# Second mixer of a hybrid decoder: the in-projection of seven heads in pairs of units, by seven half-size block products a pair

## Chip, cores and metric

The kernel runs on one core of one Trainium2 chip. The metric is device time in microseconds (us): the median of 3 runs before the change is 1518.07 us (1518.05 to 1518.93). A second number is the span of the profiled execution, from the first to the last instruction of the core.

## The reference, cut to what matters

Four sub-layers on 544 tokens (512 of a prompt, 32 of eight samples) with a model width of 1024: a Mamba-2 mixer, an MLP, an HGRN2 mixer and a second MLP, each with an RMS norm ahead and a residual add behind. The change touches the HGRN2 mixer:

```python
def hgrn_mixer(u, state, lb, w_in, norm_w, w_out):
    proj = (u @ w_in).astype(jnp.float32)
    q = jax.nn.silu(proj[..., :HGRN_F])
    fz = proj[..., HGRN_F:2 * HGRN_F]
    v = proj[..., 2 * HGRN_F:2 * HGRN_F + D_MODEL]
    g = proj[..., 2 * HGRN_F + D_MODEL:]
    logf = jnp.logaddexp(jax.nn.log_sigmoid(fz), jnp.log(jnp.maximum(lb, LB_FLOOR)) + jax.nn.log_sigmoid(-fz))
    k = (1.0 - lb) * jax.nn.sigmoid(-fz)
    ...
    o, s = hgrn_chunk_scan(q..., k..., v..., logf..., state)
    o = group_rmsnorm(o.reshape(bt, L, D_MODEL), norm_w, HGRN_N_HEADS) * jax.nn.silu(g)
    return o.astype(u.dtype) @ w_out, s
```

`u` is the normed residual, (tokens, 1024); `w_in` is (1024, 4096): q, f, v and g of 8 heads with 128 columns each. The scan runs per head.

## The kernel before

**Units and products.** The residual lies transposed in eight tiles `x[k]` of 128 x 544 (features by tokens). Weights come in units `W[u]` of 128 x 1024 f32 (512 KB): the 128 output columns of one block for all eight k-blocks. For precision a unit is split into a high part `whi` (rounded to fp32r by ScalarE, L199) and a low part `wlo` (raw minus high, VectorE, L200), in halves of 512 columns; the operand is split the same way into `uh`/`ul`. A unit takes, per k-block and half of the tokens (272), three matmuls: high by high, high by low, low by high: 8 x 3 x 2 = 48. The accumulators `ps` (pool `acc`) are two; smaller PSUM tiles come from `mx`, four. Raw units have three buffers, split halves four.

**Loads and splits.** Lists `loads` and `jobs` hold the order of all units. `load_next` (L173) issues the next load; `conv_unit` splits the next unit, a few ahead of its use. For some units ("by load") the low part is made otherwise: ScalarE writes the negative of the raw unit, rounded to the type of the tile, and GpSimd issues DMAs that add the raw weights from memory to it (`accum_op=ADD`).

**The MLPs** (`_mlp`, `seventh`) already work on pairs of units: the 2 x 2 blocks (two units by two halves of k, against two halves of k by two halves of the tokens) are multiplied by seven products of half size, named p1, p2, n6, q7, n5, p3 and q4, at slots 0, 1, 3, 4, 6, 9 and 12 of a pair, the next pair seven slots later (`SLOTS`). Their weight operands are sums of blocks (`v`, `s2`, `a22`), made by accumulating loads and by VectorE; their token operands are sums as well.

**The HGRN2 mixer** (`hgrn`) before the change: 32 units, four a head (q, f, v, g), each by `product` (48 matmuls) and `project`, which multiplies the accumulator by the row scale `hn_rb` of the RMS norm on VectorE. The operands `uh`/`ul` hold x times the norm's weight, unscaled, so they are ready before the row scale is. `head` then makes sigmoids, K and the gate. Two background queues run work beside the products: `levels` (a scan over chunk sizes 1 to 64 by doubling) and `states` (chunk states, sample states, output, group norm by `newton`, transposes, gate, split into `oh`/`ol`). `tick` counts six product steps and lets a queue step when its pace (`PACE_LEVELS`, `PACE_STATES`) is used up. At the end the out-projection takes 8 units, first with heads 0 to 3, then with heads 4 to 7. Each engine runs its instructions in the order that the program fixes; GpSimd (POOL) issues all rounding and accumulating DMAs from one in-order stream, SyncE (SP) the plain ones.

Of the kernel before, what the change touches and what calls it, by code (L numbers as in the profile page):

```python
# [16 lines left out]
P = 128  # L17
# [27 lines left out]
PACE_LEVELS, PACE_STATES = 1.8, 1.6  # L45
# [42 lines left out]


# [12 lines left out]
def trunk(ctx: ExitStack, tc: tile.TileContext, io):  # L102
# [60 lines left out]
    by_load = {ub + i for ub in (U_MLP, U_MLP2) for i in (1, 2, 3, 4, 5, 6, 8, 9)}  # L163
    plans = [plan_mlp(U_MLP, False)]
    for u in range(U_HGRN_IN, U_MLP2):
        loads.append(("u", u))
        jobs.append((("u", u), len(loads) - 1))
# [5 lines left out]
    def load_next():  # L173
        kind, u = loads[state["load"]]
        state["load"] += 1
        if kind == "u":
            raw = wraw.tile([P, 1024], F32, tag="raw", name=f"raw{u}")
            nc.sync.dma_start(raw, io["W"][u])
        elif kind == "a22":
            raw = mp["w"].tile([P, 512], F32, tag="a22", bufs=1, name=f"a22_{u}")  # L180
            nc.sync.dma_start(raw, io["W"][u + 1][:, 512:])
        else:
# [4 lines left out]
            for c in (0, 512):  # L187
                nc.gpsimd.dma_start(raw[:, c : c + 512], io["W"][u + 1][:, :512], accum_op=ADD)  # L188
# [13 lines left out]
    def conv_unit():  # L202
# [4 lines left out]
        with tc.high_priority() if u > 2 else ExitStack():  # L207
            while state["load"] <= min(at + (3 if mp else 2 if "w" in sp else 1), len(loads) - 1):
                if loads[state["load"]][0] != "u" and not mp:
                    break  # L210
                load_next()
        with tc.high_priority() if u > 2 and not mp else ExitStack():
            if kind == "u":
# [12 lines left out]
                if added(u + 1):  # L226
                    added_low(u + 1)
            else:
# [11 lines left out]
    def added_low(u):  # L240
# [5 lines left out]
        for a in range(2):  # L246
            nc.gpsimd.dma_start(lows[u][a], io["W"][u][:, 512 * a : 512 * a + 512], accum_op=ADD)

# [20 lines left out]
    def halves_of(job):  # L269
        return 2 if job[0][0] == "u" else 1  # L270
# [54 lines left out]
    def products(ps, w, ops, first, last, c0=0, step=P, run=0):  # L325
# [7 lines left out]
        for i, (k, j) in enumerate(order):  # L333
# [7 lines left out]
            if i % 6 == 5:  # L341
# [854 lines left out]
    def hgrn(then):  # L1196
        es = ExitStack()
        cp = es.enter_context(tc.tile_pool(name="h_const", bufs=1, reuse_waits="tile"))
        pool = es.enter_context(tc.tile_pool(name="h_pool", bufs=2, reuse_waits="tile"))
# [5 lines left out]
        idm = cp.tile([P, NS], F32, name="idm")  # L1205
        nc.sync.dma_start(idm, io["sel"])
# [5 lines left out]
        nc.sync.dma_start(seqrow, io["seqrow"])  # L1212
        sel = cp.tile([P, NS], F32, name="h_sel")
# [20 lines left out]
        background(rstd_steps(1.0 / D, "hn", res, nt, wait=3), "hn", wait=3)  # L1234

        def product(u):
            w = unit(u)
            ps = acc_tile(f"ps{u}")
            products(ps, w, uops, True, True)
            return ps  # L1240

        def project(u, name, ps=None):
            ps = product(u) if ps is None else ps
            t = pool.tile([P, T], F32, tag="ev", bufs=3, name=f"{name}{u}")
            nc.vector.tensor_tensor(v3(t), ps[:, :, :HF], v3(res[0]), MUL)
            return t

        def levels(h, QQ, K, f, d):


            q, Q = QQ[:, 0], QQ[:, 1]
            ac = pool.tile([P, 4, NS], F32, tag="ac", name=f"ac{h}")
# [421 lines left out]
```

## Time and profile before

| what | value |
|---|---|
| median of 3 runs | 1518.07 us |
| profiled execution, time | 1518.08 us |
| profiled execution, span | 1516.2 us |
| mean granted TensorE clock | 0.995 |
| second mixer, in-projection | 814.7 to 1087.4 us |
| second mixer, out-projection | 1087.4 to 1146 us |
| windows of that stage | PE full, DMA share 0.25 to 0.36 |

The page of the profile gives busy time by engine, a chain of waits followed back from the last instruction, groups of instructions by line and tile, and the issues of DMAs with their time to landing. Windows give the busy time of each engine, the granted clock and the DMA share in a chosen stretch. Busy times of matmuls overlap, since they are pipelined.

### The profile page before, as it was taken

Reading aid. Unit: us, or ns where it says so; the run is one execution under the profiler, and the core shown is the slowest. Engines: PE = TensorE matmul, PEld = TensorE weight load, DVE = VectorE, ACT = ScalarE, POOL = GpSimd, SP = SyncE. Lnnn points to the kernel's source line nnn. Section 1 sums busy time; section 2 is a strip of 40 time slices with the busy share of each in tenths; the row PEclk is TensorE's granted clock in tenths of the full one; section 3 lists DMA queues with packets and bytes.
Section 4 is the critical chain, followed back from the end, with each engine's and each line's share of the span. In section 5 each row is a group of like instructions: output and inputs, shape, how many; then the busy total and the mean of one; then the engine's idle time right before and its main releaser. Section 6 shows DMA issues by size and latency. Waiting matters only on the chain. (4 is left out here: it accounts for less than half of the span.)

```text
span 1516.2 us, 33202 instructions
## 1 busy us (share of the span) xinstructions
PE 1489.2 (98%) x13124; PEld 1426.4 (94%) x13124; DVE 1274.6 (84%) x2532; ACT 882.8 (58%) x1740; POOL 200.2 (13%) x289
## 2 busy tenths in 40 slices
PE   8999999999999999999999999999999999999996
PEld 7998889898999999999999999999999999999996
DVE  7989899878777879898898788888877989888895
ACT  5685756757347658575775333333336658576673
POOL 3112111120012111110100000000003111111101
PEclk9999999999999999999999999999999999999998
DMA  6366557483556576665653222233228667575741
GB/s 199 100 198 181 148 131 207 125 227 108 143 157 153 127 181 159 167 173 149 161 152 115 73 87 87 89 111 92 87 90 195 138 166 177 143 190 135 185 113 67
DMA packets 91451, 215.45 MB, mean 142 GB/s; under 512 B 16480, under 2 KB 20480, under 8 KB 91296
## 3 DMA queue, kind: packets, MB, share of 16 engines
q1 hardware_dynamic: 64688, 161.85, 32.9%
q0 software_dynamic: 25344, 50.34, 19.4%
q8 instruction: 103, 1.69, 0.4%
q10 hardware_dynamic: 1264, 1.14, 0.2%
q14 instruction: 52, 0.43, 0.1%
HBM read 196.12 MB, written 17.18 MB: 141 GB/s over the span
## 5 line engine op out<-in xcount | busy, mean ns | idle before, releaser
L199 ACT CAST whi<-raw 128x512 fp32r<-128x512 f32 x194 | 119.4, 617 | 205.9 <-PE ps L337 149.0
L200 DVE TENSOR_TENSOR wlo<-raw,whi 128x512 fp32r<-128x512 f32 x194 | 134.0, 692 | 28.4 <-ACT whi L199 26.0
L188 POOL DMA_DIRECT2D v<-in_W x94 | 82.9, 1020 | 465.2 <-DVE fl_p L200 135.4
L337 PE MATMUL ps<-uh_s,whi 128*128 128x272 f32 x576 | 124.4, 297 | 4.2 <-DVE BC L535 2.4
L337 PE MATMUL ps<-ul_s,whi 128*128 128x272 f32 x576 | 120.1, 289 | 0.0
L337 PE MATMUL ps<-uh,whi 128*128 128x272 f32 x512 | 112.4, 300 | 0.0
L337 PE MATMUL ps<-ul,whi 128*128 128x272 f32 x512 | 106.8, 289 | 0.0
L337 PE MATMUL ps<-uh,wlo 128*128 128x272 f32 x512 | 106.3, 289 | 0.0
L337 PEld LDWEIGHTS ps<-uh_s,whi 128*128 128x128 f32 x576 | 90.2, 188 | 11.9 <-issue 8.5
L337 PEld LDWEIGHTS ps<-ul_s,whi 128*128 128x128 f32 x576 | 90.4, 188 | 0.6 <-issue 0.3
L200 DVE TENSOR_TENSOR fl_p<-raw,fh_p 128x512 fp32r<-128x512 f32 x94 | 64.2, 690 | 29.1 <-ACT fh_p L199 25.6
L337 PE MATMUL ps<-uh_s,wlo 128*128 128x272 f32 x576 | 85.1, 288 | 0.0
L337 PEld LDWEIGHTS ps<-uh,whi 128*128 128x128 f32 x512 | 80.8, 189 | 3.7 <-issue 1.4
L337 PEld LDWEIGHTS ps<-ul,whi 128*128 128x128 f32 x512 | 80.4, 188 | 0.2
L337 PEld LDWEIGHTS ps<-uh,wlo 128*128 128x128 f32 x512 | 80.0, 188 | 0.2 <-issue 0.2
L199 ACT CAST fh_p<-raw 128x512 fp32r<-128x512 f32 x94 | 57.6, 620 | 38.0 <-PE pp L1108 20.2
L337 PEld LDWEIGHTS ps<-uh_s,wlo 128*128 128x128 f32 x576 | 77.2, 188 | 1.0 <-issue 0.8
L223 ACT CAST whi<-raw 128x512 fp32r<-128x512 f32 x66 | 40.6, 618 | 50.3 <-PE ps L337 21.0
L528 DVE SCALAR_TENSOR_TENSOR cacc<-pre,vh,cacc 128x568 f32<-128x568 f32 x72 | 57.9, 804 | 5.8 <-ACT cacc L526 5.3
L337 PE MATMUL po<-yh,whi 128*128 128x272 f32 x256 | 55.7, 298 | 1.2 <-ACT yh L199 1.2
L1108 PE MATMUL pc_q<-m_th,fh_q 128*128 128x272 f32 x192 | 55.3, 288 | 0.0
L1108 PE MATMUL pc_q<-m_th,fl_q 128*128 128x272 f32 x192 | 55.3, 288 | 0.0
(492 smaller groups left out, 5162.7 us busy)
## 6 DMA issues: line engine op xcount, KB each, us to landing
raw<-in_W SPq DMA_DIRECT2D x175, 512.0 KB, 4.0
v<-in_W SPq DMA_DIRECT2D x94, 256.0 KB, 4.1
v<-in_W POOLq DMA_DIRECT2D x94, 256.0 KB, 5.5
wlo<-in_W POOLq DMA_DIRECT2D x66, 256.0 KB, 6.1
a<-in_W SPq DMA_DIRECT2D x47, 256.0 KB, 4.1
w<-cum_d POOLq DMA_DIRECT2D x16, 512.0 KB, 7.5
st<-in_ssm_in SPq DMA_DIRECT2D x16, 512.0 KB, 4.5
out_ssm_s<-st SPq DMA_DIRECT2D x16, 512.0 KB, 6.1
```

The costliest lines, as they stand in the source:

```text
L188: nc.gpsimd.dma_start(raw[:, c : c + 512], io["W"][u + 1][:, :512], accum_op=ADD)
L199: nc.scalar.copy(hi, raw)
L200: (eng or nc.vector).tensor_tensor(lo, raw, hi.bitcast(F32), SUB)
L223: nc.scalar.copy(hi[a], c)
L337: nc.tensor.matmul(ps[:, h, :HF], block(a, c0 + k * step), o[:, h * HF : (h + 1) * HF], start=(first and i == 0), stop=(last and i == len( ...
L528: nc.vector.scalar_tensor_tensor(acc, pre[:, i : i + 568], vh[:, wc + 24 * i : wc + 24 * i + 1], acc, MUL, ADD)
L1108: nc.tensor.matmul(ps, block(w, k * P), o, start=(name_ in ("p1", "p2", "q7") and k == 0 and j == 0), stop=(k == 3 and j == 2), skip_group ...
```

## The change

**What it does.**
- Head 0 keeps its four whole units, with their low parts by load, and with all high products of a unit ahead of its low ones (`run=8`). So do the 8 units of the out-projection, by load.
- Heads 1 to 7 become 14 pairs, (q, f) and (v, g), by the seven products of `SLOTS`: 7 x 12 = 84 matmuls a pair in place of 96.
- The first unit of each pair is loaded by GpSimd straight into an fp32r tile ("c": the load rounds), so that p1 and p2 need no split; their low part `lo` (one buffer) is ScalarE's negative and one accumulating load of 512 KB, started by `low_ahead`, for the next pair along with n5 of the pair before. The sums `v` are made by two accumulating loads a pair, `s2` by a VectorE sum and an accumulating load. Five forms a pair are split as before.
- The row scale goes into the operands: `operands` makes n = x * weight * scale for the eight tiles, splits them (`b1`, `b2`), and makes the sums t1 to t4 in `th` and `tl`; `split_sums` splits these. Results leave PSUM by ScalarE copies (`s`, `sv`, `sw`) and half-width VectorE sums.
- The group norm's sums come from ScalarE (`accum_out`), and its power -1/2 from GpSimd (`pow`), in place of a VectorE reduction and `newton`. K is scaled on ScalarE. Paces are longer, several tiles have one buffer in place of two, and the split gate of heads 4 to 7 waits for the last pair's p1 and p3 (`late`), since it reuses the operands' tiles.

```diff
-PACE_LEVELS, PACE_STATES = 1.8, 1.6
+PACE_LEVELS, PACE_STATES = 2.6, 2.2
...
     by_load = {ub + i for ub in (U_MLP, U_MLP2) for i in (1, 2, 3, 4, 5, 6, 8, 9)}
+    by_load |= set(range(U_HGRN_IN, U_HGRN_IN + 4)) | set(range(U_HGRN_OUT, U_MLP2))
...
+    for i, u in enumerate(hgrn_pairs):
+        loads += [(kind, v) for kind, j in (("v", i), ("c", i + 1), ("va", i), ("a22", i)) for v in hgrn_pairs[j : j + 1]]
...
+        elif kind == "c":
+            raw = wraw.tile([P, 1024], F32, tag="raw", name=f"raw{u}").bitcast(F32R)
+            nc.gpsimd.dma_start(raw, io["W"][u])
...
+        elif kind == "va":
+            raw = None
+            for c in (0, 512):
+                nc.gpsimd.dma_start(loaded["v", u][:, c : c + 512], io["W"][u + 1][:, :512], accum_op=ADD)
...
+    def low_ahead(u):
+        hi = loaded["c", u]
+        lo = mp["w"].tile([P, 1024], F32R, tag="lo12", bufs=1, name=f"lo{u}")
+        nc.scalar.activation(lo, hi.bitcast(F32), AF.Copy, scale=-1.0)
+        nc.gpsimd.dma_start(lo, io["W"][u], accum_op=ADD)
+        lows[u] = lo
+
+    def pair_form(name, u):
+        i = pair_at[u]
+        if name in ("p1", "p2"):
+            c = slice(0, 512) if name == "p1" else slice(512, 1024)
+            return [loaded["c", u][:, c]], [lows[u][:, c]]
+        v = loaded["v", u]
+        if name == "n6":
+            s2 = mp["w"].tile([P, 512], F32, tag="s2", bufs=1, name=f"s2_{u}")
+            nc.vector.tensor_tensor(s2, v[:, 512:], loaded["a22", u], ADD)
+            loaded["s2", u] = s2
+        raw = {"n6": ("s2", 0), "q7": ("v", 512), "n5": ("v", 0), "p3": ("s2", 0), "q4": ("a22", 0)}[name]
...
+        split(raw, hi, lo)
+        if name == "q7":
+            nc.gpsimd.dma_start(loaded["s2", u], io["W"][u][:, 512:], accum_op=ADD)
+        if name == "n5" and i + 1 < len(hgrn_pairs):
+            low_ahead(hgrn_pairs[i + 1])
...
-        pool = es.enter_context(tc.tile_pool(name="h_pool", bufs=2, reuse_waits="tile"))
+        pool = es.enter_context(tc.tile_pool(name="h_pool", bufs=1, reuse_waits="tile"))
...
-        background(rstd_steps(1.0 / D, "hn", res, nt, wait=3), "hn", wait=3)
+        def operands():
+            yield from rstd_steps(1.0 / D, "hn", res, nt, wait=3)
+            yield 3
...
+                nc.vector.scalar_tensor_tensor(n[-1], x[j], vec[:, v0 + j : v0 + j + 1], res[0], MUL, MUL)
...
+                split(b11, *bo)
+                fops["p1", k] = bo
+                yield 1.3
...
+                split(n[1], *bo)
...
+                yield 1
...
+                nc.vector.tensor_tensor(t1, b11, b12, SUB)
+                nc.vector.scalar_tensor_tensor(t2, t1, -1.0, b22, MUL, SUB)
+                nc.vector.tensor_tensor(t3, b12, b22, SUB)
+                nc.vector.tensor_tensor(t4, b21, t2, ADD)
...
+                yield 1.4
+
+        def split_sums():
+            for k, t, (n1, n2) in sorted(sums, key=lambda e: e[0]):
...
+                split(t, *bo)
...
+                yield 0.5
...
+        def seventh(name, u):
+            if name == "p1":
+                t = acc_tile(f"hp{u}")
+                banks[u] = {"a": t[:, 0, :HF], "c": t[:, 1, :HF]}
...
+            hi, lo = take((name, u))
+            n = 0
+            for k in range(4):
+                oh, ol = fops[name, k]
+                for j, (w, o) in enumerate(((hi, oh), (hi, ol), (lo, oh))):
+                    nc.tensor.matmul(
...
+                    n += 1
+                    if n == 6:
+                        tick()
...
-            nc.vector.tensor_reduce(ms, o2, mybir.AxisListType.X, ADD)
+            for c in range(4):
+                nc.scalar.activation(o2[:, c], po[:, c * P : (c + 1) * P], AF.Square, accum_out=ms[:, c : c + 1])
...
-            r = newton(ms, 5)
+            r = pool.tile([P, 5], F32, tag="or", bufs=2, name=f"or{h}")
+            nc.gpsimd.tensor_tensor(r, ms, half, ALU.pow)
...
-        for h in range(8):
-            head(u, h)
-            u += 4
...
+        background(operands(), "hn", wait=3)
+        first = [product(u0 + i) for i in range(2)]
+        while not res:
+            step(queues[0])
+        for i in range(2):
+            project(u0 + i, first[i])
+        for i in range(2, 4):
+            project(u0 + i, product(u0 + i))
+        drain("hn")
+        background(split_sums(), "hs", q=1)
+        for name, u in hgrn_forms:
+            if name == "n6" and u == hgrn_pairs[0]:
+                drain("hs")
+            seventh(name, u)
```

**Where instructions stand.** Three places follow. In all of them, names carry a number behind the tile's own; `hn_` is the mixer's norm.

VectorE at unit 0's projection, before: behind the last step of the row scale come a weight split and the projection of q (`qz` from the accumulator `ps`), then that of f.

```order
L366 SCALAR_TENSOR_TENSOR hn_rb<-hn_rb 128x136
L200 TENSOR_TENSOR wlo_0_10787<-raw_10524,whi_0_10785 128x512
L1245 TENSOR_TENSOR qz_10768<-ps_10636,hn_rb 128x544
L1245 TENSOR_TENSOR fz_10773<-ps_10711,hn_rb 128x544
L1442 TENSOR_TENSOR q_10770<-qz_10768,q_10770 128x544
```

The same place after; the rows begin with the eighth behind the last step of the row scale (`n` are the scaled operands, `b1l`, `b2l` low parts, `th`, `tl` sums).

```order
L1326 SCALAR_TENSOR_TENSOR hn_n_10765<-x,vec,hn_rb 128x544
L1342 TENSOR_TENSOR hn_tl_10754<-hn_n_10727,hn_th_10753 128x272
L1326 SCALAR_TENSOR_TENSOR hn_n_10767<-x,vec,hn_rb 128x544
L232 TENSOR_TENSOR hn_b1l_10722<-hn_n_10765,hn_b1h_10721 128x272
L1339 TENSOR_TENSOR hn_th_10787<-hn_n_10765 128x272
L1341 TENSOR_TENSOR hn_tl_10788<-hn_n_10765,hn_n_10767 128x272
L232 TENSOR_TENSOR hn_b2l_10778<-hn_n_10767,hn_b2h_10777 128x544
L1340 SCALAR_TENSOR_TENSOR hn_th_10787<-hn_th_10787,hn_n_10767 128x272
L1407 TENSOR_TENSOR q_10799<-ps_10626,hn_rb 128x544
L1342 TENSOR_TENSOR hn_tl_10788<-hn_n_10767,hn_th_10787 128x272
L1407 TENSOR_TENSOR f_10804<-ps_10714,hn_rb 128x544
```

The projection of q has moved behind the operand work of two of the four steps of `operands`, fifteen operations in all.

TensorE at the first pair and the second, after (before, whole units follow each other here): `hp_11085` is the accumulator of the first pair, `hp_11275` that of the second, `raw_10812` the second pair's rounded unit and `lo_11090` its low part; the last product of the first pair's p2 stands five rows ahead of the first row.

```order
L1426 MATMUL hp_11085<-hn_tl_11104,fh_n_10951 128x272
L1426 MATMUL hp_11085<-hn_th_11103,fl_n_10952 128x272
L1426 MATMUL hp_11085<-hn_th_11115,fh_n_10951 128x272
L1426 MATMUL hp_11085<-hn_tl_11116,fh_n_10951 128x272
L1426 MATMUL hp_11085<-hn_th_11115,fl_n_10952 128x272
L1426 MATMUL hp_11085<-hn_th_11119,fh_n_10951 128x272
L1426 MATMUL hp_11085<-hn_tl_11120,fh_n_10951 128x272
L1426 MATMUL hp_11085<-hn_th_11119,fl_n_10952 128x272
L1426 MATMUL hp_11085<-hn_th_11147,fh_n_10951 128x272
L1426 MATMUL hp_11085<-hn_tl_11148,fh_n_10951 128x272
L1426 MATMUL hp_11085<-hn_th_11147,fl_n_10952 128x272
L1426 MATMUL hp_11275<-hn_b1h_10721,lo_11090 128x272
```

The first product with the second pair's low part comes right behind n6 of the first pair.

POOL before, at heads 1 and 2 (copies and memsets of `levels`, `values` and `states` only).

```order
L1332 COPY vr_11049<-vz_10870 128x128
L1307 COPY K_10776<-K_10776 128x96
L1307 COPY K_11200<-K_11200 128x96
L1332 COPY vr_11546<-vz_11360 128x128
L1399 MEMSET o_12460 128x128
```

POOL after, from the first pair's `s2` on (`v` are the accumulating loads of a pair's sums, `or` the power of the group norm).

```order
L311 DMA s_124_10949<-in_W 128x512
L205 DMA raw_11217<-in_W 128x1024
L291 DMA lo_11090<-in_W 128x1024
L212 DMA v_11214<-in_W 128x512 x2
L311 DMA s_126_11221<-in_W 128x512
L205 DMA raw_11444<-in_W 128x1024
L291 DMA lo_11363<-in_W 128x1024
L212 DMA v_11441<-in_W 128x512 x2
L1626 TENSOR_TENSOR or_11413<-oms_11405,h_half 128x5
```

POOL's stream now holds the loads of the pairs, and the power of head 0's group norm stands behind those of two pairs.

More of the change, by code (lines that the diff above doesn't have):

```diff
@@ L87, in _mlp_plan, with _hgrn_plan @@
     return plan
+def _hgrn_plan(ub):
+    pairs = [ub + i for i in range(4, 32, 2)]
+    forms = []
+    for i, u in enumerate(pairs):
+        for name, t in SLOTS:
+            t += 7 * i
+            forms.append((t, name, u))
+    return pairs, [x[1:] for x in sorted(forms, key=lambda x: x[0])]
 V_NMIX0, V_NMLP0, V_NMIX1, V_NMLP1, V_NF = 0, 8, 16, 24, 32
@@ L323, in block, with products @@
         return w[c // 512][:, c % 512 : c % 512 + P]
-    def products(ps, w, ops, first, last, c0=0, step=P, run=0):
+    def products(ps, w, ops, first, last, c0=0, step=P, run=0, every=6):
         n = len(ops)
@@ L340, in products @@
                 )
-            if i % 6 == 5:
+            if i % every == every - 1:
                 tick()
@@ L1212, in hgrn @@
         nc.sync.dma_start(seqrow, io["seqrow"])
+        half = cp.tile([P, 5], F32, name="h_half")
+        nc.gpsimd.memset(half, -0.5)
         sel = cp.tile([P, NS], F32, name="h_sel")
```

240 lines of the change are left out of this document (169 added, 71 removed).

## The prediction

> **What bounds the kernel now.** I read the head of the page first, then its chain of waits, then windows over the changed stage, and last single groups and the timeline.
>
> ```profile
> PE 1489.2 (98%) x13124; PEld 1426.4 (94%) x13124; DVE 1274.6 (84%) x2532; ACT 882.8 (58%) x1740; POOL 200.2 (13%) x289
> PE 1%; issue 0%; POOL 0%; POOLq 0%; ACT 0%
> ```
>
> TensorE is busy in 1489.2 of 1516.2 us. The chain covers only the end of the span and says nothing of the stage that changes, so the windows have to. Their columns: window and length, then PE, PEld, DVE, ACT and POOL busy with counts, granted clock, DMA share, GB/s.
>
> ```profile
> 600.00:700.00 100.00, 100.00 (x798) 99.77 (x797) 86.44 (x158) 65.35 (x125) 12.24 (x14) 1.00 0.58 153
> 814.70:850.00 35.30, 35.11 (x397) 33.37 (x396) 27.58 (x72) 14.68 (x27) 1.20 (x2) 1.00 0.36 119
> 884.00:918.00 34.00, 33.97 (x405) 31.79 (x405) 28.20 (x82) 12.13 (x26) 1.30 (x4) 1.00 0.31 96
> 1087.40:1146.00 58.60, 58.60 (x542) 56.39 (x541) 46.66 (x98) 24.02 (x44) 0.52 (x1) 1.00 0.32 101
> ```
>
> The second mixer runs from 814.7 to 1146 us: heads of some 34 us each, then the out-projection. PE is full at the full clock; DVE has some 6 us of 34 to spare, POOL nearly all, the DMA engines two thirds. So fewer products shorten this stage unless a new wait takes their place. The first row lies in the MLP before it, which already works with seven products a pair: PE full with DVE at 86%.
>
> **The change part by part.** *Products.* A pair of units took 2 units × 8 blocks × 3 products × 2 halves = 96 matmuls of 272 columns; seven forms of 12 make 84. Fourteen pairs save 14 × 12 = 168.
>
> ```profile
> 868.03 0.42 PE L337 MATMUL ps<-uh,wlo 128*128 128x272 f32 x2
> 868.28 0.42 PE L337 MATMUL ps<-uh,whi 128*128 128x272 f32 x2
> ```
>
> Two start every 0.25 us (the 0.42 overlap), so one is worth 0.125 us and the saving is 168 × 0.125 = **21.0 us**: a head falls from 34 to 31 us, a pair to 15.5. Head 0 and the out-projection keep their products; low parts by load only relieve a DVE that had slack there, and count nothing.
>
> *DVE in the steady part.*
>
> ```profile
> L200 DVE TENSOR_TENSOR wlo<-raw,whi 128x512 fp32r<-128x512 f32 x65 | 44.6, 687 | 6.1 <-ACT whi L199 5.2
> L1245 DVE TENSOR_TENSOR qz<-ps,hn_rb 128x544 f32<-128x544 f32 x8 | 5.8, 719 | 0.8 <-ACT hn_rb L402 0.8
> L1403 DVE TENSOR_REDUCE oms<-o 128x5 f32<-128x640 f32 x7 | 5.8, 822 | 10.9 <-ACT o L1401 10.9
> L366 DVE SCALAR_TENSOR_TENSOR nwr<-nwt,nwr 128x5 f32<-128x5 f32 x21 | 3.3, 158 | 0.1
> L1450 DVE TENSOR_SCALAR K<-nf,olb 128x544 f32<-128x544 f32 x8 | 4.0, 497 | 0.0
> L1135 DVE TENSOR_TENSOR a_p<-pc_p,s 128x272 f32<-128x272 f32 x12 | 5.2, 434 | 0.0
> ```
>
> Per head go 8 splits of 0.69, 4 scalings of 0.72, the reduction of 0.82, eleven small operations of 0.16 and the K scaling of 0.50: 11.5 us. In come 10 splits and 2 sums of 0.69 and 6 half-width operations of 0.43: 10.9 us. DVE stays at about 28 us, now of 31, or 90%. The MLP's row covers 86% at a full PE; I charge nothing, and if that cover fails, each us above 31 counts seven times. The ACT squares that accumulate, and the K scaling moved to ACT, fit into an ACT that is busy 12 of 34 us.
>
> *The start of the stage, unit 2.* DVE now makes the operands: 8 scalings, 8 splits, 16 half-width sums, and then 8 splits of the sums.
>
> ```profile
> L1011 DVE SCALAR_TENSOR_TENSOR m_n<-x,vec,m_rb 128x544 f32<-128x544 f32 x8 | 6.1, 778 | 0.0
> L200 DVE TENSOR_TENSOR m_gl<-a_n,m_gh 128x544 fp32r<-128x544 f32 x12 | 8.7, 723 | 2.5 <-ACT m_gh L199 2.1
> 814.79 0.41 PE L337 MATMUL ps<-uh,whi 128*128 128x272 f32 x2
> 825.00 0.73 PE L384 MATMUL hn_pr<-hn_rb,ident 64*128 64x136 f32 x8 [0.19 <-DVE hn_rb L366]
> 825.78 0.68 ACT L402 COPY hn_rb<-hn_pr 128x272 f32<-128x272 f32 x2 [0.78 <-PE hn_pr L384]
> 826.49 0.72 DVE L1245 TENSOR_TENSOR qz<-ps,hn_rb 128x544 f32<-128x544 f32 x1 [0.76 <-ACT hn_rb L402]
> ...
> 906.94 0.44 DVE L1296 TENSOR_TENSOR q<-q,T 128x272 f32<-128x272 f32 x1
> 907.29 0.16 DVE L364 TENSOR_TENSOR nwt<-nwr 128x5 f32<-128x5 f32 x1
> ```
>
> The order puts fifteen operand operations between the row scale and `q<-ps`, which empties the first of only two accumulators; unit 2 needs it. Before, the scale came at 826.5 and `q` followed at once. Without the weight splits among its steps (0.69 at a time) I put it at 824.8, an estimate. Behind it stand 4 scalings, 2 wide splits and 9 half-width operations: 4 × 0.70 + 2 × 0.64 + 9 × 0.36 = 7.3 us, each 0.08 less than its row, since the next one starts that much before its end (the last two rows: 0.44 long, 0.35 apart); then 0.7 for `q` itself: 832.8. Units 0 and 1 are 96 matmuls of 0.125 us, 12.0 us from 814.8; with the row-scale products beside them they end at 827.6. **PE waits 5.2 us.** With the scale as late as before it is 6.9; with one 2 us earlier, 3.2.
>
> *Level 2 of head 0.* After that `q` come 26 more DVE rows up to the level-1 results on which PE's `pa_2` rests: 5 of 0.70, 5 of 0.64, 13 of 0.36 and three small ones of 0.5 together, 11.9 us in all, so 844.7. PE arrives there after unit 2 (6.0), `pa_1` (0.4) and 28 matmuls of unit 3 (3.5), at 842.7: **2.0 us**, between 0 and 4.
>
> *The second pair's low part.* This is the one new wait of a kind that no row of before shows: `lo` has a single buffer, so ACT may write its negative only after the last product of `p2` of pair 1, POOL then issues an accumulating load of 512 KB, and PE has `p1` of pair 2 in its order only 14 matmuls and `pa_16` later, 2.0 us.
>
> ```profile
> L199 ACT CAST whi<-raw 128x512 fp32r<-128x512 f32 x194 | 119.4, 617 | 205.9 <-PE ps L337 149.0
> L1118 ACT COPY sw<-pp 128x272 f32<-128x272 f32 x21 | 7.9, 377 | 10.1 <-PE pp L1108 10.1
> L188 POOL DMA_DIRECT2D v<-in_W x94 | 82.9, 1020 | 465.2 <-DVE fl_p L200 135.4
> v<-in_W POOLq DMA_DIRECT2D x94, 256.0 KB, 5.5
> w<-cum_d POOLq DMA_DIRECT2D x16, 512.0 KB, 7.5
> ```
>
> The copy: (617 - 377) / 240 = 1.0 ns a column, so 1024 columns are 1.1 us. The issue is 1.0. The landing lies between the 5.5 of a 256 KB accumulation and two of them, 11.0; I take 7.5, the row of equal size on the same queue. That is 9.6 us against 2.0: 7.6 us of waiting. ACT also has a split ahead that waits for an accumulating load of the pair before, 0 to 4 us more; I take 1. **8.6 us**, between 5.6 and 15. The splits of the operand sums, 8 × 0.64, run inside this wait.
>
> *What a wait does to the clock.* Columns: window and length, PE busy, clock, DMA share, GB/s.
>
> ```profile
> 808.00:809.00 1.00, 0.10 (x1) 1.00 0.01 4
> 809.00:810.00 1.00, 0.75 (x3) 1.00 0.00 0
> 811.00:812.00 1.00, 0.97 (x4) 0.59 0.00 0
> 813.00:814.00 1.00, 1.00 (x6) 0.50 0.50 66
> 814.00:815.00 1.00, 1.00 (x8) 0.71 0.73 270
> ```
>
> After a gap at 808 to 810 the granted clock is about half from 811.4 to 814.5, 3.1 us, in which 1.5 us of work are lost. The waits of 5.2 and 8.6 us are longer than that gap, so I charge **2 × 1.5 = 3.0 us**, between 0 and 6.
> The Trainium skill, page "TensorE: Matmul & The Clock Gate", section "Part 1: The HAM clock gate", says that the array drops to half rate after an idle window of about 3.4 us and needs about as long at work to come back. The trace agrees, with its 3.1 us at 0.50. By the page the two waits would cost 2 × 1.7 = 3.4 us, an estimate, and the sum would end 0.4 us higher.
>
> *The steady part: low parts by the software queue.* Between the last `p2` of a pair and the next pair's `p1` stand five forms and the background work, 11 to 12.4 us; copy, issue and landing need 9.6. I charge **2 us** in all for 13 pairs; it is nothing below a landing of 8.9 us, and at 11.0 up to 2 us a pair, 26 us. Load on the DMA engines decides:
>
> ```profile
> q1 hardware_dynamic: 10809, 25.71, 34.9%
> q0 software_dynamic: 5184, 9.44, 27.6%
> 1147.00:1230.00 83.00, 81.71 (x652) 80.58 (x651) 69.06 (x134) 53.40 (x99) 19.54 (x23) 1.00 0.73 164
> wlo<-in_W POOLq DMA_DIRECT2D x15, 256.0 KB, 6.9
> ```
>
> The first two rows are of 560 to 780 us in the MLP, 220 us of 16 engines: 103 engine-us a MB by the software queue, 48 by the hardware one. After the change a pair accumulates 1.3 MB and loads 0.5 MB with rounding by software, and 1.3 MB by hardware (weights, and half a head's states): 135 + 25 to 54 + 63 = 223 to 252 of the 248 engine-us that 15.5 us hold. That is near full. The last two rows show the start of the second MLP, where a DMA share of 0.73 goes with 6.9 us a landing in place of 5.5, and still PE at 98%.
>
> *The group norm.* POOL's power takes the place of the reduction and of a chain of steps:
>
> ```profile
> 905.38 0.17 DVE L1404 TENSOR_SCALAR oms<-oms 128x5 f32<-128x5 f32 x1
> 908.15 0.15 DVE L366 SCALAR_TENSOR_TENSOR nwr<-nwt,nwr 128x5 f32<-128x5 f32 x1
> L1399 POOL MEMSET o<- 128x128 f32 x6 | 1.2, 206 | 73.8 <-PE pts L1424 73.8
> ```
>
> The power has no row: between the memset's 0.2 us and the 2.9 us from the first to the last step here. Nearest is the memset, and up to 3 us of slack a head cover it. But it stands on POOL behind loads that wait for others; `o<-po,or` waits for it on DVE, with all later splits behind. *The end:* head 7's `f` comes complete 36 matmuls (4.5 us) before the out-projection, where 96 (12 us) followed before. Together I charge **1 us**, between 0 and 12.
>
> **The sum**, against the profiled execution (1516.2 us span and 1.9 beside it, 1518.1; the runs' median is the same): -21.0 + 5.2 + 2.0 + 8.6 + 3.0 + 2.0 + 1.0 = +0.8, so 1518.9 us. The saving is real and is nearly all spent at the start.
>
> **The rivals.** *PE stays the bound (faster).* For it speaks the MLP row: the same scheme, the same operand work, PE full. If the second pair's load lands in 5.5 us and ACT isn't held, its wait is 5.6; with 3.2 at unit 2, none at level 2, one clock drop of 1.5, and nothing later, 10.3 is lost: 1507.4. Without any start loss it would be 1497.1; against it, the first MLP has more whole units ahead of its pairs than the four here.
>
> *The software queue becomes the bound (slower).* Each pair's `lo` lands later than 8.9 us and PE stands at the third product of `p1`. For it: the 223 to 252 of 248 engine-us. Against: PE at 98% in the start of the second MLP. At 10.5 us, 1.6 us a pair: 13 × 1.6 = 21 in place of 2, 1538. It decides from 0.3 us a pair on.
> A clock that dropped at every such wait, as it did after the gap at 808, would add 13 × 1.5 us more and make 1557; I give that 2 in 100, within this rival, since these waits are shorter.
> The Trainium skill, page "TensorE: Matmul & The Clock Gate", section "HAM oscillation", tells of kernels in which each wait for a load halves the clock anew; the rows above show it after one gap only.
>
> *POOL's order holds DVE (slower).* The power waits behind two issues of 1.0 us and a load of 4 to 5 us that feeds them; DVE has about 7 us of other work meanwhile. At 1.5 us beyond the slack in six heads: 9 us, 1528.
>
> **How the numbers follow.** Two executions differ by little, so I call 0.2%, 3 us, about what can be told from no change. Chances: forecast 0.34 (0.28 within, 0.03 slower, 0.03 faster), PE bound 0.33 (0.25 about 1507, 0.08 near 1497), software queue 0.21, POOL's order 0.12. Of the last two all but 0.01 are slower. Faster 0.36, same 0.29, slower 0.35. The likeliest single case is the forecast, 1518.9, by its own bounds 1513 to 1527; the range leaves out the full saving below (0.08) and the upper part of the queue's case (some 0.1): 1503 to 1538.
>
> **What would show it.** The windows of the changed kernel from 814.7 on should have PE idle about 5 us ahead of unit 2, released by DVE's `q`, and about 9 ahead of the second pair's `p1`, released by a DMA on POOL's queue, with clocks near 0.5 behind each; then heads of about 31 us with PE full. I am wrong if those gaps are missing, if a head takes 33 us or more, if `lo` lands above 9 us, or if POOL's power row starts long after its operand.

## The result, and the profile after

The change makes the kernel slower: 1531.84 us, median of 4 runs (1528.58 to 1535.19), against 1518.06; the ratio is 1.009, 95% interval 1.0067 to 1.0113. The runs of the changed kernel scatter over 6.6 us, those of the kernel before over 1 here and over up to 7 in the sets that were run beside the experiments. Beside experiment 9 one execution of it and one of the kernel before ran at a granted clock of 0.65 and 0.75 and took 2025 and 1791 us; the times and ratios below leave these two out. The profiled execution took 1532.86 us with a span of 1531.1, 14.9 us more than before.

First the head of the page of the changed kernel.

```profile
PE 1482.8 (97%) x12956; PEld 1414.5 (92%) x12956; DVE 1276.8 (83%) x2486; ACT 946.9 (62%) x1928; POOL 290.1 (19%) x392
```

TensorE runs 12956 matmuls in place of 13124: the 168 are gone. So the products were saved, and more than that was lost. The windows of the changed stage show where (window and length, then PE, PEld, DVE, ACT and POOL busy with counts, granted clock, DMA share, GB/s):

```profile
814.70:850.00 35.30, 29.81 (x311) 27.86 (x310) 30.86 (x74) 19.74 (x37) 12.18 (x19) 0.95 0.86 210
850.00:884.00 34.00, 28.28 (x276) 25.26 (x275) 22.98 (x54) 17.50 (x45) 7.02 (x10) 0.90 0.62 134
884.00:918.00 34.00, 31.05 (x396) 28.62 (x395) 27.60 (x72) 16.72 (x36) 9.17 (x13) 0.95 0.77 176
918.00:952.00 34.00, 32.98 (x417) 29.62 (x417) 29.95 (x79) 18.41 (x48) 10.96 (x14) 1.00 0.79 187
986.00:1020.00 34.00, 32.72 (x416) 29.56 (x415) 29.50 (x77) 18.60 (x49) 11.12 (x14) 1.00 0.80 191
1110.00:1160.00 50.00, 49.69 (x400) 47.61 (x399) 28.94 (x56) 28.55 (x60) 13.34 (x15) 1.00 0.69 160
```

Before, PE was full in every window. Now it idles 5.5, 5.7 and 2.9 us in the first three, 1.0 and 1.3 us in the next two and 0.3 in the last, and the clock is below 1 in the first three. A mean clock of 0.95 over 34 us is 3.4 us at half rate, 0.90 is 6.8. The timeline has the gaps of the first stretch (start, length, instruction, idle time before it and what ended it):

```profile
829.14 1.27 PE L405 MATMUL ps<-uh,wlo 128*128 128x272 f32 x8 [1.37 <-DMA wlo<-in_W]
...
834.34 0.79 PE L405 MATMUL ps<-uh,whi 128*128 128x272 f32 x2 [3.92 <-DVE q L1407]
...
855.89 0.40 PE L1426 MATMUL hp<-hn_tl,fh_n 128*128 128x272 f32 x1 [0.83 <-DVE hn_tl L232]
...
858.51 0.39 PE L1426 MATMUL hp<-hn_tl,fh_n 128*128 128x272 f32 x1 [0.71 <-DVE hn_tl L232]
...
863.20 0.59 PE L1426 MATMUL hp<-hn_b1h,lo 128*128 128x272 f32 x1 [4.17 <-DMA lo<-in_W]
...
888.47 0.60 PE L1426 MATMUL hp<-hn_b1h,raw 128*128 128x272 f32 x1 [2.95 <-DVE f L1445]
```

The waits at unit 2 (3.92) and at the second pair's low part (4.17) stand where the prediction put them. The last one is new to it: the third pair's p1 needs the accumulator that VectorE's `f` of the first pair empties, and VectorE's timeline shows why.

```profile
881.26 0.17 DVE L1624 TENSOR_SCALAR oms<-oms 128x5 f32<-128x5 f32 x1 [1.14 <-ACT o L1623]
886.10 0.69 DVE L1627 TENSOR_TENSOR o<-po,or 128x512 f32<-128x512 f32 x1 [4.67 <-POOL or L1626]
886.71 0.33 DVE L1630 TENSOR_SCALAR o<-pzs,or 32x128 f32<-32x128 f32 x1
...
888.00 0.42 DVE L1445 TENSOR_TENSOR f<-hp,sv 128x272 f32<-128x272 f32 x1
```

POOL's timeline at the same place:

```profile
883.08 1.74 POOL L212 DMA_DIRECT2D v<-in_W  x2 [8.11 <-DMA v<-in_W]
884.27 1.80 POOL L1626 TENSOR_TENSOR or<-oms,h_half 128x5 f32<-128x5 f32 x1
```

The power of head 0 stands behind two accumulating loads, which wait for the loads that they add to. VectorE waits 4.67 us for it, with `f` queued behind. In the whole stage VectorE loses this way:

```profile
DVE o L1627 <- POOL or L1626: 14.4, 8, 4.7
```

14.4 us in 8 heads. The time by stage, from the starts of instructions on TensorE's timeline (unit 0's first product, the first sample-state product `pn` of heads 2 and 6, the second MLP's first product):

| stretch | before | after |
|---|---|---|
| unit 0 to head 2's `pn` | 128.8 us | 142.5 us |
| head 2's `pn` to head 6's, per head | 35.0 us | 33.8 us |
| head 6's `pn` to the second MLP | 61.5 us | 64.0 us |
| second MLP to the end | 371.2 us | 374.8 us |

How much work lies ahead of a `pn` differs between the kernels, since the queues run at another pace; the sum of the first three rows is free of that. The second mixer as a whole went from 330.2 to 341.6 us, which is 11.4 us more where 21.0 less was to be had: 32.4 us were lost in it. 19.7 of them are idle time of PE that the kernel before does not have. For the clock, windows of 1 us show when the half rate began and ended:

```profile
833.00:834.00 1.00, 0.00 (x0) 0.00 (x0) 1.00 (x3) 0.00 (x0) 1.00 (x3) 0.88 1.12 260
837.00:838.00 1.00, 1.00 (x9) 1.00 (x9) 1.00 (x4) 1.00 (x3) 0.00 (x0) 0.91 1.12 205
...
861.00:862.00 1.00, 0.00 (x0) 0.00 (x0) 1.00 (x5) 0.00 (x0) 0.00 (x0) 0.53 0.95 176
867.00:868.00 1.00, 1.00 (x6) 1.00 (x6) 0.00 (x0) 0.00 (x0) 0.00 (x0) 0.55 0.00 0
...
888.00:889.00 1.00, 0.53 (x2) 0.53 (x3) 1.00 (x4) 0.55 (x1) 0.00 (x0) 0.69 0.37 64
891.00:892.00 1.00, 1.00 (x7) 1.00 (x7) 1.00 (x3) 0.79 (x2) 0.00 (x0) 0.61 0.95 90
```

The stretches at half rate last 3.4, 6.8 and 3.4 us, and each begins before its wait has ended: 0.6, 2.1 and 0.1 us before. The part in which PE was at work is therefore 2.8, 4.7 and 3.3 us, and half of it, 5.4 us, was lost. The other 7.3 us are what is left over: by the profile PE is busy in them. Which instructions follow each other more slowly stays open.

### The profile page after: what moved, and what is told of

Read it like the earlier page. It is cut to its first block, busy times and chain, and to the rows that moved or that the text cites. A ratio compares the mean times of both kernels' runs of the same rounds, so it can differ in the third digit from the quotient of the medians.

```text
span 1531.1 us, 33266 instructions
## 1 busy us (share of the span) xinstructions
PE 1482.8 (97%) x12956; PEld 1414.5 (92%) x12956; DVE 1276.8 (83%) x2486; ACT 946.9 (62%) x1928; POOL 290.1 (19%) x392
## 5 line engine op out<-in xcount | busy, mean ns | idle before, releaser
L231 ACT CAST whi<-raw 128x512 fp32r<-128x512 f32 x114 | 70.0, 616 | 79.1 <-PE ps L405 40.6
L256 ACT CAST whi<-raw 128x512 fp32r<-128x512 f32 x90 | 55.3, 617 | 70.2 <-PE ps L405 20.9
L232 DVE TENSOR_TENSOR wlo<-raw,whi 128x512 fp32r<-128x512 f32 x114 | 80.0, 704 | 22.1 <-ACT whi L231 20.5
L252 POOL DMA_DIRECT2D wlo<-in_W x56 | 49.1, 941 | 164.8 <-ACT wlo L251 153.6
L231 ACT CAST fh_n<-v 128x512 fp32r<-128x512 f32 x61 | 37.8, 619 | 37.2 <-PE pp L1176 32.9
L231 ACT CAST fh_p<-s 128x512 fp32r<-128x512 f32 x61 | 37.8, 620 | 34.8 <-PE pc_q L1176 27.3
L284 POOL DMA_DIRECT2D wlo<-in_W x34 | 30.1, 1044 | 146.9 <-ACT wlo L281 133.6
L232 DVE TENSOR_TENSOR fl_n<-s,fh_n 128x512 fp32r<-128x512 f32 x61 | 42.1, 690 | 16.0 <-ACT fh_n L231 11.7
L1176 PE MATMUL pp<-m_tl,fh_n 128*128 128x272 f32 x192 | 55.3, 288 | 0.0
```

The source lines that it names most:

```text
L231: nc.scalar.copy(hi, raw)
L232: (eng or nc.vector).tensor_tensor(lo, raw, hi.bitcast(F32), SUB)
L252: nc.gpsimd.dma_start(lo[a], io["W"][u][:, 512 * a : 512 * a + 512], accum_op=ADD)
L256: nc.scalar.copy(hi[a], c)
L1176: nc.tensor.matmul(ps, block(w, k * P), o, start=(name_ in ("p1", "p2", "q7") and k == 0 and j == 0), stop=(k == 3 and j == 2), skip_group ...
```

## The experiments

A ratio in what follows is to the kernel before, run on the same chip, with its 95% interval; the changed kernel has 1.009 (1.0067 to 1.0113). The intervals of experiments 1, 4, 8, 9, 10 and 11 overlap with that, so their times can't be told from the changed kernel's. Experiments 2 and 3 are slower than it, 5, 6, 7 and 12 faster.

**1. The old chain of small steps for the power.**

```diff
-            r = pool.tile([P, 5], F32, tag="or", bufs=2, name=f"or{h}")
-            nc.gpsimd.tensor_tensor(r, ms, half, ALU.pow)
+            r = newton(ms, 5)
```

> The changed kernel with its group norm's power -1/2 taken off GpSimd and made by the old chain of small VectorE steps; nothing else differs. Theory A (GpSimd's stream holds VectorE: the power stands behind issues that wait for loads, and the output scaling waits for it 1.5 us a head, 4.7 us in head 0): those waits go, the TensorE waits at pn with them, heads of 33.6 us fall by about 1 us, 1522 to 1528 us against 1531.8. Theory B (VectorE's amount of work is the bound in the steady part): eleven operations of 0.17 us more a head, 1532 to 1541 us. Theory C (the software queue's loads are the bound): no change.

1534.65 us, ratio 1.0107 (1.0081 to 1.0134): no gain. VectorE's timeline of this kernel shows that the chain is no shorter than the power:

```profile
953.25 0.16 DVE L1624 TENSOR_SCALAR oms<-oms 128x5 f32<-128x5 f32 x1
...
956.59 0.68 DVE L1626 TENSOR_TENSOR o<-po,nwr 128x512 f32<-128x512 f32 x1
```

From the mean square to the scaling are 3.3 us, where head 2 of the changed kernel took 2.2. TensorE's wait at `pn` is gone, but others came in its place, at ScalarE's `sv` (3.7 us between 880 and 1088) and at `lo` (3.2). Heads 2 to 6 took 34.1 us each. Theory B fits the time, but its reason, the amount of VectorE's work, is not shown; theory C's "no change" lies in the interval as well, and only experiment 7 speaks against it. The profiled execution, 1527.48 us, was the fastest of the four.

**2. The projection of q ahead of the operand work.**

```diff
-            nc.vector.tensor_tensor(v3(t), ps[:, :, :HF], v3(res[0]), MUL)
+            with tc.high_priority():
+                nc.vector.tensor_tensor(v3(t), ps[:, :, :HF], v3(res[0]), MUL)
```

> The changed kernel with the projections of units 0 to 3 given priority, so that q comes right behind the row scale, ahead of the fifteen operand operations. Theory A (the wait of 3.9 us at unit 2 is a matter of order): it goes and the half clock behind it too, about 5.6 us, 1526 us. Theory B (VectorE has more to do between the row scale and the first pairs than TensorE's work there covers, so the wait only moves): TensorE waits later, at the pairs' operands, by the same amount, 1530 to 1534 us.

1537.98 us, ratio 1.0151 (1.0127 to 1.0176): slower than either theory had it. TensorE's waits between 814 and 1260 us:

```profile
PE ps L405 <- DMA wlo<-in_W: 5.8, 2, 4.4
PE pa L1488 <- DVE K L1519: 5.5, 5, 2.3
PE hp L1427 <- DMA lo<-in_W: 2.7, 1, 2.7
```

The wait at unit 2 is gone, as theory A has it; what replaced it is larger, as theory B has it: unit 2's low part (4.4 us; the loads of low parts were issued from 829.0 us on, behind a load of a sum that POOL had waited 3.5 us to issue) and the first level's operands. The first stretch grew from 142.5 to 149.6 us.

**3. Eight whole units ahead of the pairs.** The number of whole units is 8 in place of 4 in the plan, the lists of loads and jobs, and `hgrn`'s loop.

```diff
-    pairs = [ub + i for i in range(4, 32, 2)]
+    pairs = [ub + i for i in range(8, 32, 2)]
...
-        for i in range(2, 4):
+        for i in range(2, 8):
             project(u0 + i, product(u0 + i))
```

> The changed kernel with eight whole units ahead of twelve pairs (heads 0 and 1 whole) in place of four ahead of fourteen. It gives back 24 matmuls, 3.0 us. Theory A (the start loses 16 us since four units cover too little of the operand work): with 24 us more of cover most of that goes, 1518 to 1524 us. Theory B (the start's loss sits at the first pairs, whatever stands ahead: the low part with one buffer, the sums, the first power): the waits move with them, 1531 to 1536 us.

1541.39 us, ratio 1.0161 (1.0144 to 1.0177), above both theories. The order of VectorE's work was not kept. The same fifteen operand operations stand ahead of q's projection, but the first pair's weight sum `s` now stands ahead of them all, and VectorE waits 9.7 us for the load of `v` that it needs; unit 2 waits three times as long as before. The first row is VectorE's:

```profile
831.30 0.69 DVE L303 TENSOR_TENSOR s<-v,a 128x512 f32<-128x512 f32 x1 [9.74 <-DMA v<-in_W]
...
840.00 0.79 PE L405 MATMUL ps<-uh,whi 128*128 128x272 f32 x2 [12.70 <-DVE q L1407]
...
907.59 0.60 PE L1426 MATMUL hp<-hn_b1h,lo 128*128 128x272 f32 x1 [3.30 <-DMA lo<-in_W]
```

The last row agrees with theory B in part: the low part's wait moved along with the pairs. But with the order changed the run doesn't tell the theories apart.

**4. The out-projection's low parts by VectorE again.**

```diff
-    by_load |= set(range(U_HGRN_IN, U_HGRN_IN + 4)) | set(range(U_HGRN_OUT, U_MLP2))
+    by_load |= set(range(U_HGRN_IN, U_HGRN_IN + 4))
```

> The changed kernel with the out-projection's eight units split by VectorE as before, no low parts by load there. Theory A (their accumulating loads delay those of the second MLP's first units, where TensorE waits 3.0 us for a low part and falls to half clock): about 4 us less, 1527 to 1529 us. Theory B (the second MLP's loads are late by themselves): 1531 to 1533 us.

1532.71 us, ratio 1.0105 (1.009 to 1.012). TensorE's wait at the second MLP's first low parts stays 3.0 us, as theory B has it; those loads are not delayed by the out-projection's.

**5. No power at all.**

```diff
-            r = pool.tile([P, 5], F32, tag="or", bufs=2, name=f"or{h}")
-            nc.gpsimd.tensor_tensor(r, ms, half, ALU.pow)
+            r = ms
```

> The changed kernel with the power of the group norm left out (the mean square itself scales the output); no step takes its place on any engine. Theory A (POOL's order is a cause): VectorE's 1.5 us a head and 4.7 us in head 0 go, TensorE's waits for f (2.9 us, and half clock behind it) and at pn go, 8 to 12 us less than the changed kernel, a ratio to before of 1.001 to 1.004. Theory B (VectorE and ScalarE are late anyway, the wait only moves, as with the small steps of VectorE): at most 3 us less, a ratio of 1.007 to 1.010.

1520.32 us, ratio 1.0023 (1.001 to 1.0036): 0.67% of 1518, 10 us, less than the changed kernel. Theory A. In the profile the mixer is 10.0 us shorter too: 3.6 in the first stretch, 5.1 in the four heads, 1.3 in the rest. The edit takes out the power's own time and its place behind the loads on POOL together. Two of the windows:

```profile
918.00:952.00 34.00, 33.84 (x454) 30.93 (x455) 30.50 (x81) 19.48 (x51) 9.83 (x14) 1.00 0.81 194
986.00:1020.00 34.00, 33.93 (x459) 30.96 (x458) 30.63 (x82) 18.37 (x46) 9.59 (x13) 1.00 0.87 203
```

PE is full again with VectorE busy 30.6 of 34 us, and heads 2 to 6 take 32.5 us each, with the same loads on the same queues at a DMA share of 0.81 to 0.87. Neither VectorE's amount of work nor the transfers held the steady part. This profiled execution, 1516.26 us, was the fastest of ten.

**6 and 7. No accumulating loads for the low parts; then none at all for the pairs.**

```diff
         nc.scalar.activation(lo, hi.bitcast(F32), AF.Copy, scale=-1.0)
-        nc.gpsimd.dma_start(lo, io["W"][u], accum_op=ADD)
```

> The changed kernel with the 14 accumulating loads of 512 KB for the pairs' low parts left out (ScalarE's negative copy stays, the low part is not made). Theory A (one buffer and its landing of 7.8 us hold the second pair): TensorE's 4.2 us there and some of the half clock behind it go, 5 to 8 us less, a ratio of 1.004 to 1.006, and heads stay at 33.5 us. Theory B (the load on the software queue holds the steady part as well): a quarter of its bytes is gone, heads fall to 32 us, 14 us less, about 1.000.

> As the last one, and the accumulating loads of the sums v and s2 of the pairs left out too: the pairs' weights are wrong sums, all engines but POOL and the DMA engines do what they did. Theory A: as without the low parts, or 1 to 2 us less. Theory B (POOL's issues and the queue's load, 0.79 of the DMA engines, hold the steady part): heads of 32 us, 6 us or more less than without the low parts alone.

The second of the two also leaves out the accumulating loads into `v` and `s2`; the rounding loads of the pairs' first units stay. 1523.48 us, ratio 1.0044 (1.003 to 1.0058), and 1519.62, ratio 1.0012 (1.0002 to 1.0022). Heads 2 to 6 take 33.3 us in both, 0.5 less than in the changed kernel, though the DMA share in the last is half of what it was:

```profile
952.00:986.00 34.00, 33.45 (x423) 30.40 (x422) 29.73 (x80) 19.14 (x47) 4.63 (x7) 1.00 0.37 112
```

So the load on the software queue is not what holds the heads, and theory A fits the first of the two. The second is 3.9 us faster than the first, more than theory A's 1 to 2 us and less than theory B's 6; its heads are those of theory A. Most of the gain lies in the first stretch: 137.2 and 130.8 us in place of 142.5, although unit 2 waits longer than in the changed kernel for q, 9.4 and 4.8 us (in the first of them the weight sum ahead of q on VectorE waits 8.2 us for its load). These edits, too, moved other instructions, so what the loads alone are worth in that stretch is not shown to the microsecond. In the last one the wait for `or` on VectorE is still there, 10.3 us in 8 heads, with hardly anything ahead of the power on POOL:

```profile
DVE o L1622 <- POOL or L1621: 10.3, 8, 1.3
```

That is 1.3 us a head from the power's own length; what the changed kernel has beyond that, 4.7 us in head 0 and 2.1 in head 2, comes with the loads ahead of it.

**8. No operand work.** `operands` makes the row scale only, and the pairs read the unscaled tiles `uh` and `ul`; `split_sums` has nothing to do.

```diff
...
+            for k in range(4):
+                a, b = uops[k], uops[k + 4]
+                fops["p1", k] = fops["n5", k] = [t[:, :HF] for t in a]
+                fops["p3", k] = fops["n6", k] = [t[:, HF:] for t in a]
+                fops["p2", k] = fops["q7", k] = [t[:, :HF] for t in b]
+                fops["q4", k] = [t[:, HF:] for t in b]
...
```

> The changed kernel without the operand work of the pairs: no scaled copies, splits or sums, the pairs read the unscaled operand tiles in their place. Theory A (the operand work is what the start's waits come from): the wait of 3.9 us at unit 2, those at the sums and the clock behind them go, and the second pair's low part comes as early as TensorE does, 10 to 16 us less, a ratio of 0.999 to 1.003, with heads still at 33.5 us. Theory B (the start is held by the chain of the low part and the first power): 4 to 6 us less, 1.005 or more.

1531.61 us, ratio 1.009 (1.0071 to 1.0108): nothing is gained, where theory A had 10 to 16 us and theory B 4 to 6. VectorE was busy 19.45 us in 814.7 to 850 in place of 30.86, and the wait at unit 2 is gone. TensorE's largest waits of this kernel:

```profile
PE pn L1612 <- DVE o L1605: 4.6, 4, 2.3
PE hp L1404 <- DMA lo<-in_W: 3.6, 1, 3.6
PE hp L1404 <- ACT sv L1417: 3.6, 1, 3.6
PE pa L1465 <- ACT K L1376: 2.3, 1, 2.3
PE ps L405 <- DMA wlo<-in_W: 2.3, 2, 2.1
```

The low part's wait and those behind the power stay, and others grew. The order moved here as well: at 832.9 us VectorE has waited 7.2 us for the load that a weight sum `s` needs, as in experiments 3 and 6, so what the operand work alone costs isn't shown. The first stretch is 138.7 us, 3.8 less; heads 2 to 6 took 34.4, with one of 36.3.

**9. A tile of its own for the second pair's low part.**

```diff
-        lo = mp["w"].tile([P, 1024], F32R, tag="lo12", bufs=1, name=f"lo{u}")
+        lo = mp["w"].tile([P, 1024], F32R, tag="hst" if pair_at[u] == 1 else "lo12", bufs=1, name=f"lo{u}")
```

> The changed kernel with the second pair's low part in a tile of its own (that of the sample states, not in use yet), so that its copy and load no longer wait for the first pair's p2; all else as it was. Theory A (the single buffer holds TensorE 4.2 us there, with half clock behind it): 4 to 8 us less than the changed kernel, a ratio of 1.004 to 1.006, like the kernel without low parts. Theory B (the low part is one of several things that are late at that place, the sums of the operands next): 0 to 3 us less, 1.007 to 1.009.

1534.66 us, ratio 1.012 (1.0097 to 1.0143), above both theories. The wait for `lo` at the second pair is gone, and unit 2's doubled:

```profile
838.11 0.80 PE L405 MATMUL ps<-uh,whi 128*128 128x272 f32 x2 [8.52 <-DVE q L1407]
...
877.51 1.08 PE L1600 MATMUL pz<-hst,o 128*32 128x128 f32 x16 [2.35 <-DMA hst<-in_hgrn_in]
```

ScalarE's copy for that low part now stands in its stream ahead of the operands' splits and waits 5.8 us there for the load of its unit; VectorE waits up to 5.4 us for these splits (`hn_b1l` for `hn_b1h`), and q's projection stands behind. The tile, too, was wanted: the sample states' load into it now comes late (second row). The wait moved to an earlier place, which theory B had in kind but not in size.

**10 and 11. The scaling of the output on ScalarE; and both of the last two.**

```diff
-            nc.vector.tensor_tensor(
-                o2[:, :4], po.rearrange("p (a b) -> p a b", b=P), r[:, :4].unsqueeze(2).to_broadcast([P, 4, P]), MUL
-            )
-            nc.vector.tensor_scalar(o2[:NS, 4], pzs[:NS, :P], r[:NS, 4:5], None, MUL)
+            for c in range(4):
+                nc.scalar.activation(o2[:, c], po[:, c * P : (c + 1) * P], AF.Copy, scale=r[:, c : c + 1])
+            nc.scalar.activation(o2[:NS, 4], pzs[:NS, :P], AF.Copy, scale=r[:NS, 4:5])
```

> The changed kernel with the scaling of the output by the group norm's power on ScalarE (five instructions a head) in place of VectorE (two); the power stays on GpSimd. Theory A (the power's 1.2 us and what stands ahead of it on POOL hold VectorE in order, and TensorE's pn behind it): VectorE's wait goes, ScalarE has 15 of 34 us to spare, heads of 32.5 to 32.8 us, 6 to 10 us less, a ratio of 1.002 to 1.005. Theory B (ScalarE's splits are held in place of VectorE's): 1.007 to 1.011.

> Both of the last two edits. If the two causes are separate, their gains add: 10 to 16 us less than the changed kernel, a ratio of 0.998 to 1.002. If one bound stands behind both, no more than the better one.

1532.12 us, ratio 1.0105 (1.0087 to 1.0123), and 1535.92, ratio 1.0127 (1.009 to 1.0163). Now ScalarE waits for the power and VectorE for ScalarE's splits; TensorE still waits at `pn`, 2.3 us in experiment 10 where the changed kernel had 2.7. Two rows of the waits of experiment 10, ScalarE's and VectorE's:

```profile
ACT o L1628 <- POOL or L1626: 9.8, 7, 5.0
DVE fl_n L232 <- ACT fh_n L231: 11.5, 12, 4.6
```

Heads 2 to 6 took 34.6 and 35.0 us. Theory B in 10, and no sum of gains in 11.

**12. The power alone, in the kernel before.**

```diff
-            r = newton(ms, 5)
+            r = pool.tile([P, 5], F32, tag="or", name=f"or{h}")
+            nc.gpsimd.tensor_tensor(r, ms, mhalf, ALU.pow)
```

> The kernel before with one part of the change alone: GpSimd's power in place of the chain of small VectorE steps in the group norm. Theory A (the power's latency costs only where VectorE has no time to spare): 28 of 34 us of VectorE work a head leave 6, nine small steps go, ratio 0.998 to 1.002. Theory B (the wait holds TensorE by the PSUM tile whatever VectorE has to spare): about 1 us a head, 1.004 to 1.007.

1514.35 us, ratio 0.9986 (0.9975 to 0.9996): not slower, and the only version that ends a little ahead of the kernel before. A window and VectorE's wait for the power there:

```profile
884.00:918.00 34.00, 34.00 (x424) 31.85 (x422) 27.03 (x70) 12.54 (x27) 3.21 (x4) 1.00 0.32 104
...
DVE o L1409 <- POOL or L1408: 9.4, 7, 1.4
```

VectorE waits 1.3 us a head, as in experiment 7, and TensorE doesn't notice: PE stays full, and heads keep their 35.0 us. Theory A.

## Why the prediction was right and wrong

The time lies in the range, but 13 us above the forecast of "nearly all spent at the start" and outside the 1513 to 1527 of that case; the range reached it only through the two slower rivals. Two of the four signs of being wrong came: heads of 33 us or more (33.8), and a power row that starts long after its operand (2.8 us in head 0). By the prediction's steps:

- **Products.** Right in number: 168 matmuls less, 0.125 us apart where nothing interrupts. The "heads of about 31 us" were not: 34 us is a mean over the whole stage, heads 2 to 6 took 35.0 before, so with 24 matmuls (3.0 us) less 32.0 were to be had. With PE full in experiment 5 they took 32.5, so some 0.5 us a head of the saving did not come even there, for a reason that stays open. The changed kernel's 33.8 hold 1.0 us of idle time and 0.8 of work beyond the 32.0.
- **VectorE in the steady part.** Right in amount: 30.6 of 34 us, 90%, with PE full in experiment 5.
- **Unit 2.** Place right, 5.2 us forecast; 3.92 there and 1.37 just before it at unit 1's low part. The reason for the wait holds, since without any operand work (experiment 8) it goes; as a price it is not borne out, since the time stays, though in another order of VectorE's work.
- **Level 2 of head 0.** The 2.0 us did not come there; 1.5 us came a little later, at the sums' splits.
- **The second pair's low part.** Place and mechanism right, 8.6 forecast, 4.17 measured: TensorE arrived 4.9 us behind the last product of p2 in place of 2.0, 1.5 of them by the waits at the sums' splits, so less of the load was left to wait for. The 7.5 us taken for the landing was near the 7.8 of the group.
- **The clock.** 3.0 forecast for two waits, 5.4 measured for three: 1.4, 2.3 and 1.7 us at the waits of 3.9, 4.2 and 2.9. The stretch that the price was taken from, at 811 us in the kernel before, was 3.4 us long and not 3.1: the 0.59 of its first row is 0.8 us at half rate, the 0.71 of its last is 0.6, with two full ones between. TensorE had been idle only 0.95, 0.21 and 0.37 us ahead of it, so that row gave the length of a stretch and not how long a wait must be.
- **The software queue.** A small price was right, 2 forecast, no wait for `lo` seen in the steady part of the changed kernel; as a rival it falls by experiments 5 and 7. The DMA engines were busy 0.8 in the steady windows, not the 0.9 to 1.0 worked out:

```profile
q0 software_dynamic: 11197, 27.72, 52.9%
lo<-in_W POOLq DMA_DIRECT2D x14, 512.0 KB, 7.8
```

  The first row is of 815 to 1090 us: 0.529 x 275 x 16 / 27.72 = 84 engine-us a MB where 103 was taken.
- **The group norm.** This step failed: "Nearest is the memset, and up to 3 us of slack a head cover it." The power takes 1.2 us, not 0.2, and the slack of up to 3 us a head did not cover it: TensorE waited 2.7 us at `pn` and 2.9 for `f`. Charged with 1 us together with the end, the power with its place on POOL is worth 10 us by experiment 5. The rival "POOL's order holds DVE", 1528, named the engine and nearly the price; but most of the wait is the power's own length (1.3 us a head with POOL nearly empty, experiment 7), and the loads ahead of it add only in some heads, head 0 above all.
- **The second MLP.** Not in the sum, 3.6 us: one wait of 3.0 us for a low part and half clock behind it. In the profiles of the changed kernel's family that wait is between 0.4 us (experiment 5) and 3.8 (experiment 9), and experiment 4 rules out the out-projection's loads. What decides it stays open.

So the loss of 32.4 us in the stage has two main parts that were shown by taking them away, each without its repair being found: the power with its place on POOL (10 us) and the pairs' accumulating loads (12 us by the ratio; in the profile 14.0 us of the mixer, 11.7 of them in the first stretch, by low parts, the loads ahead of head 0's power, and the clock). They can't be added: head 0's wait for the power, with `f` and the half clock behind it, goes in both, and no run leaves out both. I treated the waits as a sum of separate prices. Experiments 1, 2, 8, 9, 10 and 11 each removed a wait that the profile shows (10 only one of VectorE's), and each time another one came or grew. Taking out a whole latency helped (5, 6, 7); moving it to another engine didn't. Why heads in experiments 1, 8, 10 and 11 take 34 to 35 us, more than in the changed kernel, was not settled.

## What to carry to other kernels

When TensorE's work between two fixed points shrinks, look whether every chain beside it still fits the shorter time, and not only each engine's sum: VectorE's wait of 1.3 us a head for the power cost nothing at 35 us (experiment 12), and the power, waited for 1.4 us a head behind head 0, cost about 1.3 us a head in the changed kernel (33.8 against the 32.5 of experiment 5). That the shorter head is the reason is argued and not shown: the changed kernel also has fewer buffers, more work on ScalarE, and VectorE's work in another order, and no run separates these. A small operation on another engine is priced by the round trip, from its operand's last writer to the reader that stands next in order, and by what that in-order stream holds ahead of it. And before a wait is repaired by moving work, look what stands behind the new place: leaving the work out altogether first tells about what the repair could gain, as long as the other instructions keep their order (in experiments 3, 6 and 8 they did not).

## What was not expected of the hardware

GpSimd's power on 128x5 values takes 1.2 us, more than the 0.9 to 1.0 us of a DMA's issue there and twelve times the 0.10 us of a memset of the same size (`oms`, 128x5, in the changed kernel). The tile's row of experiment 12 has name, count, and shortest, median and longest in ns:

```profile
L1408 POOL TENSOR_TENSOR or<-oms,h_half x7: 1166/1167/1207, 871.2 to 1081.0; 128x5 f32<-128x5 f32 x7
```

The half clock began within each of the three longest waits, 3.3, 2.0 and 2.9 us after TensorE fell idle, and lasted 3.4 or 6.8 us, so that these 11.0 us of waiting cost another 5.4. And a load of 512 KB that accumulates landed in 7.8 us, where one of 256 KB took 5.7 in the same stretch.
